# A low-rank update on one core: equal groups of 8 tiles, two spaces for the narrowed copy, and a written order on every engine

## The chip, the cores and the metric

The kernel runs on one core of a Trainium2 chip. A core has TensorE (PE in the profile; PEld is its weight load), VectorE (DVE), ScalarE (ACT), GpSimd (POOL) and SyncE (SP), each with its own instruction queue, 16 DMA engines, and two on-chip memories: SBUF, and PSUM, into which TensorE writes its results. The metric is the device time of one execution in microseconds (us); lower is better.

## The reference

The result is x plus a scaled product of x with two thin matrices (rank 16):

```python
batch, seq, d_model, r = 16, 512, 768, 16
# x: (16, 512, 768) float32, A: (768, 16), B: (16, 768), scale = 0.5
def reference(x, A, B, scale):
    lora = np.matmul(np.matmul(x, A), B)
    return (x + scale * lora).astype(np.float32)
```

There are 8192 rows of 768 numbers. x is 25.17 MB and the output as much, so 50.3 MB cross between the chip's main memory and SBUF.

## The kernel before

**Tiles and parts.** A tile is 128 rows of 768 numbers; there are 64. They come in six parts of 8, 8, 16, 16, 8 and 8 tiles (`PARTS`). A part is loaded into one SBUF space, updated there in place, and stored from there. The spaces are named a, b, c, d; parts 4 and 5 use a and b again (`ROOM`), so they can be loaded only when parts 0 and 1 have been stored. All loads of x and all stores are issued on SP's queue in the order: loads of part 0 (in two halves, `LOADS`), 1, 2 and 3; then stores 0 and 1; then loads 4 and 5, each waiting for the landing of the store that frees its space; then stores 2 to 5. A store waits until every tile of its part is summed.

**The steps of a group.** The work on tiles goes in groups of 4, 12, 16, 16 and 16 (`GROUPS`), and each passes six steps:

1. *narrowed* (L114): four tiles at a time are copied from float32 to float16 into `xh`; ACT and POOL take turns. `xh` is one space of 16 tiles that every group uses again.
2. *turned* (L118): DVE transposes each four tiles of `xh` in place, as 32x32 blocks of 4-byte pairs.
3. *projected* (L129): PE multiplies by A, 24 matmuls per group into one PSUM bank (`ps_yt`); each has 32 columns per tile, so 128, 384 or 512 columns.
4. *spread* (L140): ACT copies the result, scaled, into the diagonal blocks of `y_bd`, four copies per group. There are two `y_bd`, used in turn.
5. *raised* (L150): for two tiles at a time PE multiplies by B, four matmuls into `lora_ps`. A `lora_ps` takes three PSUM banks and there are two of them, so a raise waits for the sum two before it.
6. *added* (L157): DVE adds `lora_ps` to the two tiles of x in place. When a part's last pair is summed, *finished* (L162) issues its store.

Before the first group, A is brought into block form (L97, L102 into `w_bd`) and B is copied four times into `b_mm` (L107), all on DVE.

**What sets the order.** The program is written in an order of its own (the list `order` at L181 mixes turns "t" with sums "a"), and the framework's planner then arranges the instructions of each engine by its own estimates, within what the data allow. In the built program DVE does the four b_mm copies ahead of the transposition of A. For the last two groups it does four sums, two turns, three sums, two turns and the last sum. The projection of the next group follows its last turn.

Of the kernel before, what the change touches and what calls it, by code (L numbers as in the profile page):

```python
# [9 lines left out]
MM_DT = mybir.dt.float16  # L10


PARTS = [8, 8, 16, 16, 8, 8]

ROOM = ["a", "b", "c", "d", "a", "b"]

LOADS = {0: [4, 4]}


GROUPS = [4, 12, 16, 16, 16]  # L20

SUB = 4


@with_exitstack
def kernel(
    ctx: ExitStack,
    tc: tile.TileContext,
    x: bass.AP,
    A: bass.AP,  # L30
    B: bass.AP,
    scale: bass.AP,
    out: bass.AP,
):
    nc = tc.nc
    fp32 = mybir.dt.float32
    P = 128
    Q = 32

    x2 = x.flatten_outer_dims()  # L40
    out2 = out.flatten_outer_dims()
    T, D = x2.shape
    R = A.shape[1]
    NC = D // 64
    GMAX = max(GROUPS)
    assert sum(PARTS) * P == T and sum(GROUPS) == sum(PARTS)
    sc = float(scale)

    const = ctx.enter_context(tc.tile_pool(name="const", bufs=1))
    xpool = ctx.enter_context(tc.tile_pool(name="xp", bufs=1))  # L50
    ypool = ctx.enter_context(tc.tile_pool(name="yp", bufs=1))
    ps_y = ctx.enter_context(tc.tile_pool(name="ps_y", bufs=2, space=bass.MemoryType.PSUM))
    ps_l = ctx.enter_context(tc.tile_pool(name="ps_l", bufs=2, space=bass.MemoryType.PSUM))

    parts = []
    where = []
    tok = 0
    for i, S in enumerate(PARTS):
        parts.append([None, tok, S])
        where += [(i, s) for s in range(S)]  # L60
        tok += S * P

    def rows(t2, i):
        _, tok0, S = parts[i]
        return t2[ds(tok0, S * P), :].rearrange("(p s) d -> p s d", s=S)

    def loaded(i):
        S = parts[i][2]
        t = xpool.tile([P, S, D], fp32, name=f"x_sb{i}", tag=ROOM[i])
        parts[i][0] = t  # L70
        end = 0
        for w in LOADS.get(i, [S]):
            nc.sync.dma_start(out=t[:, ds(end, w), :], in_=rows(x2, i)[:, ds(end, w), :])
            end += w

    a_rows = const.tile([Q, 64 * R], fp32, name="a_rows")
    a_t = const.tile([Q, 2, R, Q], fp32, name="a_t")
    b_f32 = const.tile([R, D], fp32, name="b_f32")  # L80
    w_bd = const.tile([P, NC, 2, P], MM_DT, name="w_bd")
    b_mm = const.tile([P, D], MM_DT, name="b_mm")
    xh = const.tile([P, GMAX, D], MM_DT, name="xh")
    y_bd = [const.tile([P, GMAX, P], MM_DT, name=f"y_bd{i}") for i in range(2)]

    nc.vector.memset(a_rows, 0.0)  # L86
    loaded(0)
    nc.scalar.dma_start(out=b_f32, in_=B)
    nc.scalar.dma_start(out=a_rows[0:NC, :], in_=A.rearrange("(c e) r -> c (e r)", e=64))
    for i in range(1, 4):  # L90
        loaded(i)
    nc.gpsimd.memset(w_bd.rearrange("p c k m -> p (c k m)").bitcast(fp32), 0.0)  # L92
    nc.gpsimd.memset(b_mm.bitcast(fp32), 0.0)  # L93
    for t in y_bd:
        nc.gpsimd.memset(t.rearrange("p s m -> p (s m)").bitcast(fp32), 0.0)  # L95

    nc.vector.transpose(  # L97
        out=a_t.rearrange("i k r c -> i (k r) c"),
        in_=a_rows.rearrange("c (i k r) -> c (k r) i", k=2, r=R),
    )  # L100
    for b in range(P // Q):
        nc.vector.tensor_copy(  # L102
            out=w_bd[ds(b * Q, Q), :, :, ds(b * Q, R)],
            in_=a_t[:, :, :, 0:NC].rearrange("i k r c -> i c k r"),
        )
    for b in range(P // Q):
        nc.vector.tensor_copy(out=b_mm[ds(b * Q, R), :], in_=b_f32)  # L107

    starts = [sum(GROUPS[:g]) for g in range(len(GROUPS))]

    def narrowed(g, q):
        i, s = where[starts[g] + q * SUB]
        engine = nc.gpsimd.tensor_copy if q % 2 else nc.scalar.copy
        engine(out=xh[:, ds(q * SUB, SUB), :], in_=parts[i][0][:, ds(s, SUB), :])  # L114

    def turned(q):
        v = xh[:, ds(q * SUB, SUB), :].bitcast(fp32)
        nc.vector.transpose(out=v, in_=v)  # L118

    state = {}  # L120

    def projected(g, steps):
        n = GROUPS[g]
        if g not in state:
            state[g] = ps_y.tile([P, GMAX * Q], fp32, name="ps_yt")
        xv = xh.rearrange("p s (c j k) -> p s c j k", c=NC, k=2)
        for m in steps:
            c, k = divmod(m, 2)
            nc.tensor.matmul(  # L129
                state[g][:, 0 : n * Q].rearrange("p (s j) -> p s j", j=Q),  # L130
                w_bd[:, c, k, :], xv[:, 0:n, c, :, k],
                start=(m == 0), stop=(m == 2 * NC - 1),
            )

    def spread(g):
        n = GROUPS[g]
        y = state.pop(g).rearrange("p (s j) -> p s j", j=Q)
        for b in range(P // Q):
            q = ds(b * Q, Q)
            nc.scalar.mul(out=y_bd[g % 2][q, 0:n, q], in_=y[q, 0:n, :], mul=sc)  # L140

    lora = {}

    def raised(g, p):
        t = ps_l.tile([P, 2, D], fp32, name="lora_ps")
        lora[g, p] = t
        for h in range(2):
            lhsT = y_bd[g % 2][:, 2 * p + h, :]
            for n0, w in ((0, 512), (512, 256)) if h == 0 else ((0, 256), (256, 512)):
                nc.tensor.matmul(  # L150
                    t[:, h, ds(n0, w)], lhsT, b_mm[:, ds(n0, w)], start=True, stop=True
                )

    def added(g, p):
        i, s = where[starts[g] + 2 * p]
        xs = parts[i][0][:, ds(s, 2), :]
        nc.vector.tensor_tensor(out=xs, in0=xs, in1=lora.pop((g, p)), op=mybir.AluOpType.add)  # L157

    def finished(g, p):
        i, s = where[starts[g] + 2 * p]  # L160
        if s + 2 == PARTS[i]:
            nc.sync.dma_start(out=rows(out2, i), in_=parts[i][0])  # L162
            if i == 1:
                loaded(4)
                loaded(5)

    MMS = 2 * NC
    last = len(GROUPS) - 1
    for q in range(GROUPS[0] // SUB):
        narrowed(0, q)  # L170
        turned(q)
    projected(0, range(MMS))
    spread(0)
    raised(0, 0)
    for g in range(len(GROUPS)):
        pairs = GROUPS[g] // 2
        subs = GROUPS[g + 1] // SUB if g < last else 0
        for q in range(subs):
            narrowed(g + 1, q)

        order = ["a", "a"]  # L181
        p_left, q_left = pairs - 2, subs
        while q_left or p_left:
            if q_left:
                order.append("t")
                q_left -= 1
                if q_left == subs - 1 and q_left and p_left:
                    order.append("t")
                    q_left -= 1
            if p_left:  # L190
                order.append("a")
                p_left -= 1
        p = q = 0
        done = 0
        after = 0
        rest = sum(1 for o in order[max(i for i, o in enumerate(order) if o == "t"):] if o == "a") if subs else 0
        for o in order:
            if o == "t":
                turned(q)
                q += 1  # L200
                continue
            if p + 1 < pairs:
                raised(g, p + 1)
            if q == subs and subs:
                after += 1
                to = min(MMS, -(-MMS * after // max(1, rest - 1)))
                projected(g + 1, range(done, to))
                done = to
            added(g, p)
            finished(g, p)  # L210
            p += 1
        if subs:
            projected(g + 1, range(done, MMS))
            spread(g + 1)
            raised(g + 1, 0)


# [33 lines left out]
```

## Time and profile before

| what | value |
|---|---|
| median of 3 runs | 143.31 us (142.47 to 144.72) |
| the profiled execution | 142.38 us, its span 140.6 us |
| busy: PE, DVE, ACT, POOL | 61.6, 87.5, 35.7, 22.8 us |
| sums (L157) | 32, mean 1.741 us |
| turns (L118) | 16, mean 1.750 us |
| projection matmuls (L129) | 120, 30.4 us in all |
| raising matmuls (L150) | 128, 31.8 us in all |
| narrowing casts on ACT and POOL (L114) | 9 and 7, 2.75 us each |
| first and last store issued | 39.9 and 129.9 us |
| bytes moved by DMA | 50.47 MB, mean 359 GB/s over the span |

The span reaches from the first to the last instruction; the time of an execution is a little longer. The profile's second part cuts the span into 40 slices of 3.5 us: a digit is the busy share of an engine in tenths, and the rows that begin with DMA and GB/s tell how busy the 16 DMA engines were and what they moved. A line of the costliest groups names the source line, the engine, the operation, the tiles and the count; then busy time and mean duration in ns; then how long the engine stood idle just before these instructions and what ended most of that wait. The chain is followed back from the last instruction to whatever released each step. The granted clock is the share of full speed that TensorE was given.

### The profile page before, as it was taken

Reading aid. Unit: us, or ns where it says so; the run is one execution under the profiler, and the core shown is the slowest. Engines: PE = TensorE matmul, PEld = TensorE weight load, DVE = VectorE, ACT = ScalarE, POOL = GpSimd, SP = SyncE. Lnnn points to the kernel's source line nnn. Section 1 sums busy time; section 2 is a strip of 40 time slices with the busy share of each in tenths; the row PEclk is TensorE's granted clock in tenths of the full one; section 3 lists DMA queues with packets and bytes.
Section 4 is the critical chain, followed back from the end, with each engine's and each line's share of the span. In section 5 each row is a group of like instructions: output and inputs, shape, how many; then the busy total and the mean of one; then the engine's idle time right before and its main releaser. Section 6 shows DMA issues by size and latency. Waiting matters only on the chain.

```text
span 140.6 us, 687 instructions
## 1 busy us (share of the span) xinstructions
PE 61.6 (44%) x248; PEld 26.8 (19%) x248; DVE 87.5 (62%) x58; ACT 35.7 (25%) x30; POOL 22.8 (16%) x15
## 2 busy tenths in 40 slices
PE   0000740195553039757049984450709927842000
PEld 0000620042220013223013432220203413320000
DVE  2659059800699991039999771999995008999000
ACT  2070197004960000299000019910000060000000
POOL 8200061004910000292000009400000000000000
PEclk9999999559999856985555799996555895599555
DMA  5999999999999799999998009999005999579992
GB/s 126 382 422 441 447 447 447 447 447 447 447 447 447 336 440 396 413 343 413 447 440 357 0 0 447 447 447 447 0 2 224 433 452 447 238 329 447 447 447 119
DMA packets 1931, 50.47 MB, mean 359 GB/s; under 512 B 236, under 2 KB 236, under 8 KB 264
## 3 DMA queue, kind: packets, MB, share of 16 engines
q1 hardware_dynamic: 1872, 50.33, 84.7%
q10 hardware_dynamic: 56, 0.10, 0.3%
q8 instruction: 2, 0.03, 0.1%
q14 instruction: 1, 0.01, 0.0%
HBM read 25.26 MB, written 25.17 MB: 359 GB/s over the span
## 4 chain that ended last, share of the span: by engine, by line
DVE 51%; PE 25%; ACT 6%; DMA 5%; issue 4%; DVEq 1%; ACTq 0%
DVE x_sb L157 29%; PE ps_yt L129 21%; DVE xh L118 19%; ACT y_bd L140 6%; DMA a_rows<-in_A_dram 5%; PE lora_ps L150 4%; DVE a_t L97 1%; DVE w_bd L102 1%; DVEq L246 1%; DVE a_rows L86 1%; ACTq L246 0%; ACTq L140 0%; DVEq L97 0%; ACTq L114 0%
## 5 line engine op out<-in xcount | busy, mean ns | idle before, releaser
L157 DVE TENSOR_TENSOR x_sb<-x_sb,lora_ps 128x1536 f32<-128x1536 f32 x32 | 54.2, 1741 | 36.8 <-PE lora_ps L150 36.8
L150 PE MATMUL lora_ps<-b_mm,y_bd 128*128 128x512 f16 (+1 forms) x128 | 31.8, 387 | 32.3 <-DVE x_sb L157 21.4
L129 PE MATMUL ps_yt<-xh,w_bd 128*128 128x512 f16 (+2 forms) x120 | 30.4, 424 | 33.5 <-DVE xh L118 33.5
L114 POOL CAST xh<-x_sb 128x3072 f16<-128x3072 f32 x7 | 19.1, 2749 | 66.1 <-PE ps_yt L129 31.8
L140 ACT ACTIVATE y_bd<-ps_yt 32x512 f16<-32x512 f32 (+2 forms) x20 | 10.1, 503 | 73.1 <-PE ps_yt L129 72.9
L118 DVE STREAM_TRANSPOSE xh<-xh 128x1536 f32<-128x1536 f32 x16 | 27.4, 1750 | 0.0
L114 ACT CAST xh<-x_sb 128x3072 f16<-128x3072 f32 x9 | 24.4, 2750 | 4.2 <-DMA x_sb<-in_x_dram 4.1
L150 PEld LDWEIGHTS <-y_bd 128*128 128x128 f16 x128 | 13.6, 110 | 50.4 <-issue 33.9
L129 PEld LDWEIGHTS <-w_bd 128*128 128x128 f16 x120 | 13.2, 119 | 49.8 <-issue 22.7
L107 DVE CAST b_mm<-b_f 16x768 f16<-16x768 f32 x4 | 2.2, 550 | 2.8 <-DMA b_f<-in_B_dram 2.7
L97 DVE STREAM_TRANSPOSE a_t<-a_rows 32x1024 f32<-32x1024 f32 x1 | 1.9, 1932 | 1.6 <-DMA a_rows<-in_A_dram 1.6
L102 DVE CAST w_bd<-a_t 32x384 f16<-32x384 f32 x4 | 1.9, 472 | 0.1
L114 ACT ACT_TABLE_LOAD x1 | 1.3, 1283 | 2.5 <-DVE a_rows L86 2.5
L95 POOL MEMSET y_bd<- 128x1024 f32 x2 | 1.8, 956 | 0.0
L86 DVE MEMSET a_rows<- 32x1024 f32 x1 | 0.9, 912 | 1.0 <-PEq L232 1.0
L92 POOL MEMSET w_bd<- 128x1536 f32 x1 | 1.4, 1378 | 0.3 <-POOLq L232 0.3
L93 POOL MEMSET b_mm<- 128x384 f32 x1 | 0.4, 419 | 0.0
L232 POOL MEMSET const-float32-0.0<- 128x1 f32 x1 | 0.1, 99 | 0.2 <-issue 0.2
L232 POOL MEMSET const-bfloat16-1.0<- 128x1 bf16 x1 | 0.1, 102 | 0.0
L232 POOL MEMSET const-uint8-127<- 128x1 uint8 x1 | 0.1, 102 | 0.0
L232 POOL MEMSET const-float32-1.0<- 128x1 f32 x1 | 0.1, 99 | 0.0
## 6 DMA issues: line engine op xcount, KB each, us to landing
x_sb<-in_x_dram SPq DMA_DIRECT2D x2, 6144.0 KB, 38.1
out_dram<-x_sb SPq DMA_DIRECT2D x4, 3072.0 KB, 10.1
out_dram<-x_sb SPq DMA_DIRECT2D x2, 6144.0 KB, 16.9
x_sb<-in_x_dram SPq DMA_DIRECT2D x3, 3072.0 KB, 16.5
x_sb<-in_x_dram SPq DMA_DIRECT2D x2, 1536.0 KB, 8.7
b_f<-in_B_dram ACTq DMA_DIRECT2D x1, 48.0 KB, 3.8
a_rows<-in_A_dram ACTq DMA_DIRECT2D x1, 48.0 KB
```

The source lines that it names most:

```text
L86: nc.vector.memset(a_rows, 0.0)
L95: nc.gpsimd.memset(t.rearrange("p s m -> p (s m)").bitcast(fp32), 0.0)
L97: nc.vector.transpose(out=a_t.rearrange("i k r c -> i (k r) c"), in_=a_rows.rearrange("c (i k r) -> c (k r) i", k=2, r=R),)
L102: nc.vector.tensor_copy(out=w_bd[ds(b * Q, Q), :, :, ds(b * Q, R)], in_=a_t[:, :, :, 0:NC].rearrange("i k r c -> i c k r"),)
L107: nc.vector.tensor_copy(out=b_mm[ds(b * Q, R), :], in_=b_f32)
L114: engine(out=xh[:, ds(q * SUB, SUB), :], in_=parts[i][0][:, ds(s, SUB), :])
L118: nc.vector.transpose(out=v, in_=v)
L129: nc.tensor.matmul(state[g][:, 0 : n * Q].rearrange("p (s j) -> p s j", j=Q), w_bd[:, c, k, :], xv[:, 0:n, c, :, k], start=(m == 0), stop= ...
L140: nc.scalar.mul(out=y_bd[g % 2][q, 0:n, q], in_=y[q, 0:n, :], mul=sc)
L150: nc.tensor.matmul(t[:, h, ds(n0, w)], lhsT, b_mm[:, ds(n0, w)], start=True, stop=True)
L157: nc.vector.tensor_tensor(out=xs, in0=xs, in1=lora.pop((g, p)), op=mybir.AluOpType.add)
L246: with _tile.TileContext(nc) as tc:
```

## The change

The groups become eight equal ones of 8 tiles. The narrowed copy gets two spaces of 8 tiles, used in turn by even and odd groups, so that it takes as much SBUF as before. Each `y_bd` shrinks to 8 tiles. Part 2 is loaded in two halves of 8 tiles. Above all, from the preparation of A and B onward the planner is switched off (`tc.manual_schedule()`): every engine executes its instructions in the order in which the program writes them. DVE's b_mm copies therefore stand behind those into `w_bd`.

In the written order the casts of a group stand two groups ahead of its sums. DVE does the two turns of group g+1 before the four sums of group g. PE does two raises, then a third of the next group's 24 projection matmuls, a raise, a third, a raise and the last third. The projection matmuls have 256 columns now, and there are 192 in place of 120. The spread of group g+1 follows the sums of group g; on ACT it stands behind the cast of group g+2.

```diff
-LOADS = {0: [4, 4]}
-GROUPS = [4, 12, 16, 16, 16]
+LOADS = {0: [4, 4], 2: [8, 8]}
+GROUP = 8
...
-    xh = const.tile([P, GMAX, D], MM_DT, name="xh")
-    y_bd = [const.tile([P, GMAX, P], MM_DT, name=f"y_bd{i}") for i in range(2)]
+    xh = [const.tile([P, GROUP, D], MM_DT, name=f"xh{i}") for i in range(2)]
+    y_bd = [const.tile([P, GROUP, P], MM_DT, name=f"y_bd{i}") for i in range(2)]
+
+    ctx.enter_context(tc.manual_schedule())
...
+    def narrowed(g):
+        for q in range(GROUP // SUB):
+            i, s = where[g * GROUP + q * SUB]
+            engine = nc.gpsimd.tensor_copy if q % 2 else nc.scalar.copy
+            engine(out=xh[g % 2][:, ds(q * SUB, SUB), :], in_=parts[i][0][:, ds(s, SUB), :])
+
+    def turned(g):
+        for q in range(GROUP // SUB):
+            v = xh[g % 2][:, ds(q * SUB, SUB), :].bitcast(fp32)
+            nc.vector.transpose(out=v, in_=v)
...
+    THIRD = MMS // 3
+    narrowed(0)
+    narrowed(1)
+    turned(0)
     projected(0, range(MMS))
     spread(0)
+    for g in range(NG):
+        more = g + 1 < NG
+        raised(g, 0)
+        raised(g, 1)
+        if g + 2 < NG:
+            narrowed(g + 2)
+        if more:
+            turned(g + 1)
+        added(g, 0)
+        if more:
+            projected(g + 1, range(0, THIRD))
+        raised(g, 2)
+        added(g, 1)
+        if more:
+            projected(g + 1, range(THIRD, 2 * THIRD))
+        raised(g, 3)
+        added(g, 2)
+        if more:
+            projected(g + 1, range(2 * THIRD, MMS))
+        added(g, 3)
+        finished(g)
+        if more:
             spread(g + 1)
```

## The prediction

> **What bounds the kernel now.** I read the page's busy shares, slices and chain first, then the costliest groups, the chain in order of time, and the DMA engines stretch by stretch.
>
> ```profile
> PE 61.6 (44%) x248; PEld 26.8 (19%) x248; DVE 87.5 (62%) x58; ACT 35.7 (25%) x30; POOL 22.8 (16%) x15
> ...
> DVE  2659059800699991039999771999995008999000
> ...
> DMA  5999999999999799999998009999005999579992
> GB/s 126 382 422 441 447 447 447 447 447 447 447 447 447 336 440 396 413 343 413 447 440 357 0 0 447 447 447 447 0 2 224 433 452 447 238 329 447 447 447 119
> ...
> DVE 51%; PE 25%; ACT 6%; DMA 5%; issue 4%; DVEq 1%; ACTq 0%
> DVE x_sb L157 29%; PE ps_yt L129 21%; DVE xh L118 19%; ACT y_bd L140 6%; DMA a_rows<-in_A_dram 5%; PE lora_ps L150 4%; DVE a_t L97 1%; DVE w_bd L102 1%; DVEq L246 1%; DVE a_rows L86 1%; ACTq L246 0%; ACTq L140 0%; DVEq L97 0%; ACTq L114 0%
> ```
>
> No engine is near full: DVE is busiest with 62%. The DMA row is near full up to slice 21 (from 0, 3.5 us each) and then falls to zero twice, in 22 to 23 and 28 to 29; full slices move 447 GB/s. The chain is half DVE (sums L157, turns L118) and a quarter PE, nearly all of it the projection L129.
>
> ```profile
> L157 DVE TENSOR_TENSOR x_sb<-x_sb,lora_ps 128x1536 f32<-128x1536 f32 x32 | 54.2, 1741 | 36.8 <-PE lora_ps L150 36.8
> L150 PE MATMUL lora_ps<-b_mm,y_bd 128*128 128x512 f16 (+1 forms) x128 | 31.8, 387 | 32.3 <-DVE x_sb L157 21.4
> L129 PE MATMUL ps_yt<-xh,w_bd 128*128 128x512 f16 (+2 forms) x120 | 30.4, 424 | 33.5 <-DVE xh L118 33.5
> ...
> L118 DVE STREAM_TRANSPOSE xh<-xh 128x1536 f32<-128x1536 f32 x16 | 27.4, 1750 | 0.0
> L114 ACT CAST xh<-x_sb 128x3072 f16<-128x3072 f32 x9 | 24.4, 2750 | 4.2 <-DMA x_sb<-in_x_dram 4.1
> ```
>
> DVE lost 36.8 us ahead of sums, waiting for the raising matmuls, and PE lost 33.5 us ahead of projections, waiting for DVE's turns. They take turns at waiting. The chain in order of time (start, length, what) shows one such handover whole:
>
> ```profile
> 102.28 3.42 DVE xh L118 x2
> ...
> 105.75 7.36 PE ps_yt L129 x24
> ...
> 113.14 0.59 ACT y_bd L140
> ...
> 115.58 0.84 PE lora_ps L150 x4
> ...
> 116.44 11.74 DVE x_sb L157 x7
> ```
>
> The last turn ends at 105.70, then 24 projection matmuls (7.36 us), the spreading copies (2.4 us) and a raise (0.84 us) pass before DVE adds again at 116.44. DVE had one sum left to fill that time and sat idle for 9.1 us of it. The chain of a group is thus bare once per group. What that costs shows in the DMA queue (busy time by engine, then granted clock, share of the DMA engines, GB/s):
>
> ```profile
> 47.00:76.80 29.80, 16.15 (x51) 6.04 (x52) 20.93 (x13) 7.76 (x6) 5.44 (x2) 0.64 1.00 419
> 76.80:84.90 8.10, 7.15 (x30) 2.98 (x28) 5.50 (x4) 0.91 (x2) 0.89 (x1) 0.86 0.12 49
> 84.90:97.80 12.90, 4.71 (x24) 2.33 (x25) 10.51 (x7) 6.85 (x5) 4.56 (x2) 0.93 1.07 461
> 97.80:108.20 10.40, 5.33 (x14) 1.80 (x14) 9.53 (x6) 0.00 (x0) 0.00 (x0) 0.50 0.00 1
> ...
> 124.00:138.10 14.10, 1.75 (x9) 0.67 (x7) 5.84 (x4) 0.00 (x0) 0.00 (x0) 0.72 1.04 444
> ```
>
> There is no load left to move after 76.8, and a store goes out only when its whole part is summed. A packet is counted where it starts, and one of 48 KB takes 1.76 us at a sixteenth of 447 GB/s (one of 24 KB half of that). So the queue stands still from 77.6 to 84.9, 99.5 to 108.2 and 123.1 to 124.1: 7.3 + 8.7 + 1.0 = 17.0 us. The kernel is bounded by DVE's and PE's alternation from about 77 us on, and by the DMA engines before that.
>
> **The change, part by part.**
>
> *The order on DVE.* Each group of 8 now needs two turns and four sums. Turns that stand behind one another are 1.70 us apart (3.42 for two), sums 1.67 (6.75 for four): 10.1 us a group, as long as nothing is late. Behind the turns of group g+1 stand the four sums of group g, so projection and spreading of g+1 have 6.7 us of sums and then 3.4 us of the turns of g+2 to hide in.
>
> *PE in a group.* Four raises at 0.82 us are 3.3 us. No row has matmuls of 256 columns: 128 columns take 2.72/24 = 0.113 us, and 384 run at 0.164 us apart at full clock, 0.32 at half. So 24 cost between 2.7 and 3.9 us at full clock; I take 3.0, nearer the 128 row since a weight load (0.110 us) lies in each. At half clock, by the 0.427 us spacing of 512 columns at 51.6 us, 24 x 0.427/2 = 5.1 us, and four raises at 1.44 us are 5.8 us. That is 6.3 us a group at full clock, 10.9 at half, against DVE's 10.1. At full clock the last third ends 1.5 us before the last sum does, the spread (four copies between the 268 and 482 ns of the 128 and 384 rows, so 1.1 to 1.9 us, taken 1.5) and a raise end 1.0 us after it, and the turns cover that. In PE's queue the third and fourth raise stand behind projection thirds that wait for the turns; those are done before the first sum starts, so they hold nobody. The shorter groups raise the spreads from 20 copies (10.1 us) to 32 (12.0 us), all on ACT, which is 25% busy.
>
> *Two spaces for the narrowed copy.* POOL waited 31.8 us for projections to leave the single space. Now a cast waits for the projection two groups back, done a group earlier. The cast of g+2 stands ahead of the spread of g+1 on ACT, so a late load also delays that spread. Casts now run beside turns, which no row here shows. Beside sums POOL's casts kept 2.75 us and sums 1.75 us, so I take 0; if the two excluded each other wholly, 2.75 us a group would come on top. It cannot gain: turns alone already take 1.75 us.
>
> *The start.* The planner had put the four b_mm casts (2.24 us) into DVE's wait for A; in written order they stand behind w_bd and end at 14.65 instead of 12.39. The second half of part 0 lands at 11.4 and POOL's cast of it ends at 14.2, so the turns of group 0 run 14.65 to 18.05, its projection to 21. ACT is held by the cast of part 1 (lands 18.8, cast to 21.55), so the spread ends at 23.1. DVE turns group 1 from 21.6 to 25.0 and adds until 31.7. The first store, issued at 39.9 before, goes out at about 32.
>
> *Part 2 in two loads.* One more issue on SP (0.42 us), and the first half lands at about (18.8 + 33.9)/2 = 26.4, midway between part 1 and the whole of part 2; cast by 29.2, needed at 31.7. Without it group 2 would wait 5 us.
>
> *From there.* DVE ends groups 1 to 4 at 41.8, 51.9, 62.0 and 72.1. Group 4 needs part 3, which lands at 48.1, cast 50.9, needed 51.9: no wait. Loads 4 and 5 wait on SP for the landings of stores 0 and 1. The DMA queue serves in order (store 0, issued at 39.93, moved only when the loads were through at 47, and landed at 55.0), so an earlier issue does not bring load 4 in before the 71.1 of now. Its cast ends at 73.85, DVE waits 1.8 us; groups 5, 6, 7 end at 84, 94 and 102.
>
> *The transfers, which set the end.* Stores go out at 32, 42, 64 (behind load 5's issue on SP), 84, 94 and 102. Until 76.8 the queue carries what it carries now, without a hole. Then 18.87 MB of stores remain, and the queue gets to them at 77, 91, 105 and 112: each is issued 7 to 13 us before its turn. So the three gaps go and nothing is late next but the queue itself. Sum by gaps: 140.6 - 17.0 = 123.6. Sum by pace: 18.87 MB at 447 GB/s (slices of full stores) is 42.2 us, from 77.6 to 119.8, and 1.6 us from last byte to the end of the span as now: 121.4. I take the middle, 122.5. The profiled execution of before took 142.38, 1.78 over its span, so **124.3 us**. It was 0.9 under the median of 143.31; the forecast lies 13% under either, and 2% is about what a measurement here tells from no change. At the 418 GB/s of the stretch that mixes loads and stores, 18.87 MB take 45.1 us and the time is 126.1; at the 461 of 84.9 to 97.8 it is 122.
>
> **Rivals.**
>
> *The clock stays half and PE sets the pace.* Granted clock in two stretches:
>
> ```profile
> 62.00:79.00 17.00, 10.46 (x30) 3.69 (x28) 16.71 (x10) 4.59 (x2) 2.25 (x1) 0.50 0.87 372
> 79.00:96.10 17.10, 9.66 (x49) 4.53 (x48) 12.32 (x8) 7.76 (x6) 5.44 (x2) 1.00 0.75 322
> ```
>
> The clock was half for 17 us while PE was busy 62% of them, and full in the next 17 us with 56%: it depends on how idle time is placed. It fell at 62.0 after 2.5 us of idleness. The new order has 62% at full clock, with holes of 1.5 to 1.7 us. If it falls, a group takes 10.9 us of PE plus the bare spread of 1.6: 12.5. If all groups do so, DVE ends at 21.6 + 8 x 12.5 = 121.6, and 10.7 us from the last store's issue to the end as now (140.6 - 129.9): 132.3, **134 us**. Against it: at half clock PE would be busy 87% of the time, and such a stretch (120 to 123.4) was followed by full clock. Up to 1.2 us more a group is covered by the 7 us ahead of store 3. A full exclusion of casts and turns comes to the same place: 21.6 + 8 x 12.9 + 10.7 + 1.8 = 137.
>
> *The transfers keep a mean of 359 GB/s.* That is the page's mean over the span; if it were a ceiling of the memory, 50.47 MB would take 140.6 us and nothing would change: **142 us**. The Trainium skill, in "DMA: Bandwidth & Descriptors", section "Where 436 GB/s comes from", says just this, that between HBM and SBUF the memory side binds, at about 358 GB/s a core; by that the change gains nothing. The trace disagrees: 419 GB/s over the 29.8 us from 47.0, 461 in 84.9 to 97.8, 444 in 124.0 to 138.1.
>
> *Slower: the group's steps stay bare in written order.* PE's queue holds the raises behind thirds that wait for turns, and ACT's holds the spread behind a cast that may wait for a load. If turns, projection at half clock, spread, raise and the first two sums followed each other, a group would take 3.4 + 5.1 + 1.5 + 1.4 + 3.3 = 14.7 us; from 87.3 to 116.4 before took 29.1 us for 16 tiles, 14.6 for 8. Then 21.6 + 8 x 14.6 + 10.7 + 1.8 = **151 us**. It decides from 13.5 us a group on: 21.6 + 8 x 13.5 = 129.6 is when DVE ends now. For it: 51 of the first 130 us ran at half clock. Against it: casts are due a whole group early but for load 4, and the turns no longer wait for sums.
>
> That the change does not do what it says is excluded on DVE: in the built program two turns stand ahead of each four sums.
>
> **How the numbers follow.** Full DMA queue, 122 to 127: 0.74. Half clock or blocked casts, in part or all along, 127 to 137: 0.17. The 359 GB/s ceiling: 0.04. Bare steps, slower: 0.03. The rest, 0.02, is faster than 122. The range of 121.5 to 131 takes in the first case and the nearer half of the second. Faster by over 2%: 0.93; within: 0.04; slower: 0.03.
>
> **What would show it.** The DMA row at nines from slice 1 to the last but one, with no gap over 1 us; the first store issued near 32 and the last near 102; DVE's idle time before sums down from 36.8 to under 8 us; a period of about 10.1 us between groups; load 4 landing near 71 with a short wait of DVE behind it; turns still at 1.75 us beside casts. Wrong would be a period over 11.3 us (store 3 late for the queue), transfers under 418 GB/s once stores follow each other, or the clock at half for most of the span.

## The result

The changed kernel takes 125.28 us (median of 4 runs, 124.99 to 125.44) against 143.16 us before: 0.876 of the time, 95% interval 0.872 to 0.880. The forecast was 124.3, and the time lies inside its range. The profiled execution took 125.14 us, its span 123.3.

The page of the changed kernel, with the rows that answer to those shown of before:

```profile
PE 51.8 (42%) x320; PEld 32.3 (26%) x320; DVE 89.8 (73%) x58; ACT 35.3 (29%) x41; POOL 25.1 (20%) x16
...
DVE  2019997826999999999989999999998499000000
...
DMA  4999999999998897999999999989989989999980
GB/s 73 398 371 466 406 454 414 454 430 391 510 510 383 383 499 335 430 414 454 414 446 422 422 454 507 407 383 494 449 351 478 478 351 446 391 438 438 414 375 32
...
DVE 57%; PE 12%; issue 6%; DMA 5%; ACT 2%; DVEq 1%; ACTq 0%
```

The DMA row has no zero left before its last slice: it is at nine, or close to it, from slice 1 to slice 38. DVE is busy 73% of the span in place of 62%, and from slice 11 to slice 30 it hardly stops. PE's busy time fell by 9.8 us although it does the same multiplications. The chain now ends with DVE's last sum and 57% of it is DVE, but that is not what binds: the last store was issued at 105.15 and landed 17.4 us later, because the queue had other stores to move first.

The costliest groups of the changed kernel:

```profile
L155 DVE TENSOR_TENSOR x_sb<-x_sb,lora_ps 128x1536 f32<-128x1536 f32 x32 | 54.0, 1741 | 6.2 <-PE lora_ps L148 6.2
L129 PE MATMUL ps_yt<-xh,w_bd 128*128 128x256 f16 x192 | 28.8, 299 | 31.1 <-DVE xh L119 31.1
L148 PE MATMUL lora_ps<-b_mm,y_bd 128*128 128x512 f16 (+1 forms) x128 | 26.1, 338 | 19.7 <-ACT y_bd L138 13.8
...
L119 DVE STREAM_TRANSPOSE xh<-xh 128x1536 f32<-128x1536 f32 x16 | 27.4, 1754 | 1.0 <-ACT xh L114 1.0
```

The wait that bound the kernel, DVE ahead of its sums, fell from 36.8 to 6.2 us. PE still waits 31.1 us for turns, of which 21.1 us is the start; the rest comes in pieces of up to 1.8 us while DVE does the turns.

DVE in the changed kernel, in order of time (start, length, what, count):

```profile
35.46 3.43 DVE L119 STREAM_TRANSPOSE xh<-xh 128x1536 f32<-128x1536 f32 x2
38.82 6.71 DVE L155 TENSOR_TENSOR x_sb<-x_sb,lora_ps 128x1536 f32<-128x1536 f32 x4
45.45 3.42 DVE L119 STREAM_TRANSPOSE xh<-xh 128x1536 f32<-128x1536 f32 x2
48.79 6.71 DVE L155 TENSOR_TENSOR x_sb<-x_sb,lora_ps 128x1536 f32<-128x1536 f32 x4
55.42 3.42 DVE L119 STREAM_TRANSPOSE xh<-xh 128x1536 f32<-128x1536 f32 x2
58.77 5.05 DVE L155 TENSOR_TENSOR x_sb<-x_sb,lora_ps 128x1536 f32<-128x1536 f32 x3
```

Sums start at 38.82, 48.79 and 58.77: a group takes 9.97 us, with no idle time shown between its pieces.

The DMA engines of the changed kernel, stretch by stretch (busy time by engine, granted clock, DMA share, GB/s):

```profile
4.00:46.00 42.00, 17.04 (x106) 11.05 (x107) 32.56 (x24) 15.51 (x16) 11.25 (x4) 1.00 1.03 438
...
48.00:76.00 28.00, 17.43 (x112) 11.05 (x111) 27.50 (x18) 12.62 (x15) 8.25 (x3) 0.94 1.01 433
76.00:104.00 28.00, 16.22 (x96) 9.60 (x96) 25.72 (x17) 5.89 (x10) 2.75 (x1) 0.94 1.03 443
```

In three long stretches the queue moved 433 to 443 GB/s, whether loads, loads mixed with stores, or stores alone.

### The profile page after: what moved, and what is told of

Read it like the earlier page. It is cut to its first block, busy times and chain, and to the rows that moved or that the text cites. A ratio compares the mean times of both kernels' runs of the same rounds, so it can differ in the third digit from the quotient of the medians.

```text
span 123.3 us, 854 instructions
## 1 busy us (share of the span) xinstructions
PE 51.8 (42%) x320; PEld 32.3 (26%) x320; DVE 89.8 (73%) x58; ACT 35.3 (29%) x41; POOL 25.1 (20%) x16
## 4 chain that ended last, share of the span: by engine, by line
DVE 57%; PE 12%; issue 6%; DMA 5%; ACT 2%; DVEq 1%; ACTq 0%
DVE x_sb L155 31%; DVE xh L119 19%; PE ps_yt L129 8%; DMA a_rows<-in_A_dram 5%; PE lora_ps L148 5%; DVE w_bd L103 3%; ACT y_bd L138 2%; DVE b_mm L108 2%; DVE a_t L98 2%; DVEq L225 1%; DVE a_rows L87 1%; ACTq L225 0%; ACTq L138 0%; DVEq L103 0%; DVEq L98 0%
## 5 line engine op out<-in xcount | busy, mean ns | idle before, releaser
L129 PE MATMUL ps_yt<-xh,w_bd 128*128 128x256 f16 x192 | 28.8, 299 | 31.1 <-DVE xh L119 31.1
L148 PE MATMUL lora_ps<-b_mm,y_bd 128*128 128x512 f16 (+1 forms) x128 | 26.1, 338 | 19.7 <-ACT y_bd L138 13.8
L114 POOL CAST xh<-x_sb 128x3072 f16<-128x3072 f32 x8 | 22.2, 2781 | 56.2 <-DMA x_sb<-in_x_dram 49.7
L129 PEld LDWEIGHTS <-w_bd 128*128 128x128 f16 x192 | 20.2, 105 | 39.4 <-issue 33.3
L114 ACT CAST xh<-x_sb 128x3072 f16<-128x3072 f32 x8 | 22.0, 2752 | 23.8 <-DMA x_sb<-in_x_dram 23.7
L138 ACT ACTIVATE y_bd<-ps_yt 32x256 f16<-32x256 f32 x32 | 12.0, 375 | 35.9 <-PE ps_yt L129 35.3
L148 PEld LDWEIGHTS <-y_bd 128*128 128x128 f16 x128 | 12.1, 100 | 30.6 <-ACT y_bd L138 16.1
L103 DVE CAST w_bd<-a_t 32x384 f16<-32x384 f32 x4 | 4.3, 1087 | 0.1
L96 POOL MEMSET y_bd<- 128x512 f32 x2 | 1.0, 528 | 0.0
## 6 DMA issues: line engine op xcount, KB each, us to landing
x_sb<-in_x_dram SPq DMA_DIRECT2D x1, 6144.0 KB, 45.6
```

The source lines that it names most:

```text
L103: nc.vector.tensor_copy(out=w_bd[ds(b * Q, Q), :, :, ds(b * Q, R)], in_=a_t[:, :, :, 0:NC].rearrange("i k r c -> i c k r"),)
L114: engine(out=xh[g % 2][:, ds(q * SUB, SUB), :], in_=parts[i][0][:, ds(s, SUB), :])
L129: nc.tensor.matmul(y_ps[g], w_bd[:, c, k, :], xv[:, :, c, :, k], start=(m == 0), stop=(m == 2 * NC - 1),)
L138: nc.scalar.mul(out=y_bd[g % 2][q, :, q], in_=y[q, :, :], mul=sc)
L148: nc.tensor.matmul(t[:, h, ds(n0, w)], lhsT, b_mm[:, ds(n0, w)], start=True, stop=True)
```

## The experiments

The kernel before was run beside each set; its medians there were 144.0 (the first four runs), 143.3 (the next four) and 143.3 us (the last four). Ratios are to those.

### Is the queue now the only bound?

The first run keeps the loads of x and the stores in SP's order and leaves out everything else, the small loads of A and B too, so its output is x itself:

```diff
     for i in range(1, 4):
         loaded(i)
... (removed: preparation, casts, turns, matmuls, spreads and sums of all groups)
+    for i in range(len(PARTS)):
+        nc.sync.dma_start(out=rows(out2, i), in_=parts[i][0])
+        if i == 1:
+            loaded(4)
+            loaded(5)
```

> The changed kernel's loads and stores in its order on SP's queue, and nothing else: no cast, turn, matmul or sum, so the output is x itself. Theory (from the first load on the DMA queue alone sets the time of the changed kernel): 123 to 126 us, within 2% of its 125.3. Rival (DVE's chain of groups still sets part of it): under 120 us, since no store waits for a sum here.

Measured: 123.01 us (122.94 to 123.06). All the computing of the changed kernel thus adds 2.3 us to its bare transfers; before it added about 20. The theory holds.

The second run issues the stores on ACT's queue:

```diff
-        nc.sync.dma_start(out=rows(out2, i), in_=parts[i][0])
+        nc.scalar.dma_start(out=rows(out2, i), in_=parts[i][0])
```

> As the run with the transfers alone, but the stores are issued on ACT's queue, so that loads and stores no longer stand in one line; the output is x itself. Theory (the 16 DMA engines' pace binds, at about 438 GB/s): the same within 1%, 123 to 126 us. Rival (one queue leaves holes where one transfer follows another): 2 to 5% quicker, 117 to 122 us.

Measured: 123.20 us (123.06 to 123.31). A second queue closes no holes, so the bound is not that loads and stores stand in one line. What is left is the pace at which the 16 engines move the data; whether the engines or the memory behind them set that pace was not tried.

### How much delay of DVE does the queue cover?

An unused tile is turned once more behind each group's two turns, once 512 numbers wide, once 1536:

```diff
+    pad = const.tile([P, 512], fp32, name="pad")    # 1536 in the second run
...
             nc.vector.transpose(out=v, in_=v)
+        nc.vector.transpose(out=pad, in_=pad)
```

> The changed kernel with one more turn of an unused tile of 512 numbers behind each group's two turns, about 0.6 us of DVE time, 4.8 us in all. Theory (the DMA queue sets the end and store 3 is issued 5.4 us before its turn): it is late by 0.6 x 7 = 4.2 us, still covered, 125 to 126 us. Rival (DVE sets the end): 130 us.

> The same with one full turn (1536 numbers) more in each group, 1.7 us, 13.4 us in all, a period of 11.7 us. Theory (queue, 5.4 us of cover at store 3): store 3 is 11.9 us late, a hole of 6.5 us, and all later stores stay covered: 131 to 133 us. Rival (DVE sets the end): 138 to 139 us. Rival (DVE is far from mattering): 125 to 126 us.

Measured: 125.19 us (124.96 to 125.60) and 128.93 us (128.22 to 130.40). The small delay costs nothing. The large one costs about 3.5 us of the 13.4 that DVE was given; the expected 131 to 133 was too high. DVE and the queue in that run, from two views, show why:

```profile
27.51 6.75 DVE L159 TENSOR_TENSOR x_sb<-x_sb,lora_ps 128x1536 f32<-128x1536 f32 x4 [0.67 <-PE lora_ps L152]
...
87.72 5.04 DVE L159 TENSOR_TENSOR x_sb<-x_sb,lora_ps 128x1536 f32<-128x1536 f32 x3
93.22 1.75 DVE L159 TENSOR_TENSOR x_sb<-x_sb,lora_ps 128x1536 f32<-128x1536 f32 x1 [0.46 <-PE lora_ps L152]
```

```profile
91.50:95.00 3.50, 2.57 (x18) 1.66 (x16) 3.04 (x3) 0.78 (x3) 0.00 (x0) 0.88 0.03 14
95.00:125.00 30.00, 11.00 (x56) 6.10 (x56) 18.46 (x11) 2.22 (x6) 0.00 (x0) 0.74 0.98 419
```

The hole is there, but it is 3.5 us long and not 6.5. Store 3 was issued at 95.01 and not at 97.9. Of the seven added turns ahead of it the first two fell into waits that DVE has at the start of the changed kernel anyway (0.98 us ahead of its second pair of turns, 3.42 us ahead of its first sums), and the first sums started at 27.51 here, before the 28.80 there. From then on five added turns cost 10.2 us, a little more than their 8.5. The cover at store 3 was sized rightly; the delay was not.

### What closed the gaps: order, spaces or group size?

Three parts of the change were undone one at a time, the place of the turns in two ways. In the kernel before, groups of 8 were made alone, and then together with a second space.

The planner left on:

```diff
-    ctx.enter_context(tc.manual_schedule())
```

> The changed program with the planner left on, so that groups of 8, two spaces and the written program stay and only the order on the engines is the planner's: it does the b_mm copies first and does the turns of two groups in a row ahead of eight sums. Theory (turns ahead of the neighbour's sums keep the queue fed, whoever orders them): 125 to 129 us. Rival (the gain comes from the hand-written order on each engine): 135 us or more.

Measured: 125.45 us (124.97 to 126.58), ratio 0.875 [0.867, 0.883]. Switching the planner off is worth nothing that can be measured: given this program it also sets turns ahead of sums.

The turns of the next group behind the four sums:

```diff
-        if more:
-            turned(g + 1)
         added(g, 0)
...
         added(g, 3)
         finished(g)
         if more:
+            turned(g + 1)
+            projected(g + 1, range(MMS))
             spread(g + 1)
```

> The changed kernel with the two turns, the whole projection of the next group and its spread moved behind the four sums. Theory (the gain comes from hiding projection, spread and raise behind sums): a group takes 6.7 + 3.4 + 2.7 to 5.1 + 1.6 + 0.8 to 1.4 = 15.2 to 18.2 us, DVE ends at 28 + 7 x that + 6.7, and 12.5 us come behind it: 154 to 175 us, slower than the kernel before. Rival (small groups, two spaces and the split load bring the gain): under 135 us.

Measured: 164.27 to 168.11 us in four runs, ratio 1.144 [1.131, 1.157]. DVE waits 7.1 to 7.4 us for a raise in each group of the middle of this run. With the whole chain bare once in every 8 tiles the small groups are a loss.

The turns between the second and the third sum:

```diff
+        added(g, 0)
+        raised(g, 2)
+        added(g, 1)
+        raised(g, 3)
         if more:
             turned(g + 1)
-        added(g, 0)
... (removed: the sums, raises and thirds that followed here)
+            projected(g + 1, range(MMS))
         added(g, 2)
...
         added(g, 3)
```

> The changed kernel, two spaces and written order, with the turns of the next group between the second and the third sum and the whole projection behind them, as the program of the kernel before has them. Theory (with two spaces the place of the turns decides): only two sums, 3.4 us, lie over projection, spread and raise (5.1 us at full clock, 8.1 at half), so a group takes 12 to 15 us; DVE ends near 119 to 139, 131 to 151 us. Rival (two spaces are enough wherever the turns stand): within 2% of 125.3.

Measured: 142.08 us, ratio 0.992 [0.988, 0.996]. Two sums don't cover the chain. From DVE's order of time in this run, where the bracket gives its idle time and what ended it:

```profile
69.16 3.42 DVE L155 TENSOR_TENSOR x_sb<-x_sb,lora_ps 128x1536 f32<-128x1536 f32 x2 [3.62 <-PE lora_ps L148]
72.49 3.43 DVE L119 STREAM_TRANSPOSE xh<-xh 128x1536 f32<-128x1536 f32 x2
75.84 3.38 DVE L155 TENSOR_TENSOR x_sb<-x_sb,lora_ps 128x1536 f32<-128x1536 f32 x2
82.83 3.42 DVE L155 TENSOR_TENSOR x_sb<-x_sb,lora_ps 128x1536 f32<-128x1536 f32 x2 [3.60 <-PE lora_ps L148]
```

DVE waits 3.6 us for a raise once a group, and a group takes 13.67 us.

One space for the narrowed copy, with the turns left ahead. The casts of a group must then follow the projection of the one before it:

```diff
-    xh = [const.tile([P, GROUP, D], MM_DT, name=f"xh{i}") for i in range(2)]
+    xh = [const.tile([P, GROUP, D], MM_DT, name=f"xh{i}") for i in range(1)]
...
-        if g + 2 < NG:
-            narrowed(g + 2)
...
             spread(g + 1)
+            if g + 2 < NG:
+                narrowed(g + 2)
```

> The changed kernel with one space of 8 tiles for the narrowed copy: the casts of the next group follow the projection of the one before it, and on ACT they follow its spread. Theory (the two spaces take the casts off the chain): turns wait for a cast that ends 2.9 us after the last sum, 13 us a group, sums of group 0 from about 34: DVE ends near 127, 137 to 141 us. Rival (the order of turns and sums alone brings the gain): within 2% of 125.3.

Measured: 143.36 us, ratio 0.998 [0.992, 1.003]: the whole gain is gone, a little more than expected. DVE in order of time in this run:

```profile
71.15 3.44 DVE L119 STREAM_TRANSPOSE xh<-xh 128x1536 f32<-128x1536 f32 x2 [3.48 <-ACT xh L114]
74.51 6.85 DVE L155 TENSOR_TENSOR x_sb<-x_sb,lora_ps 128x1536 f32<-128x1536 f32 x4
84.85 3.44 DVE L119 STREAM_TRANSPOSE xh<-xh 128x1536 f32<-128x1536 f32 x2 [3.48 <-ACT xh L114]
```

Now the turns of each group wait 3.48 us for ACT's cast, and a group takes 13.7 us again. Not all of that wait comes from the space, as ACT shows ahead of the turn at 71.15:

```profile
66.81 1.54 ACT L138 ACTIVATE y_bd<-ps_yt 32x256 f16<-32x256 f32 x4 [9.42 <-PE ps_yt L129]
...
68.37 2.75 ACT L114 CAST xh<-x_sb 128x3072 f16<-128x3072 f32 x1
```

The projection is done by 66.8, and the cast then stands 1.54 us behind the spread on ACT. About 1.9 us of the wait is what the one space costs by itself; the other 1.5 us is this order on ACT. With the cast first the turns could start some 1.5 us earlier in each group, roughly 10 us over seven groups. That is an estimate from these rows; the run was not made, so 143.36 us is the time of one space in this order and not the best that one space can give.

The kernel before with groups of 8, and then with two spaces as well:

```diff
-GROUPS = [4, 12, 16, 16, 16]
+GROUPS = [8] * 8
```

> The kernel before with groups of 8 and nothing else changed: one space, its own order, the planner. Theory (small groups alone bring little, since a cast must wait for the one space and the turns stand between two and two sums): 12.6 to 15.6 us a group, 134 to 145 us. Rival (small equal groups alone bring the gain, because stores go out in smaller steps): 130 us or less.

```diff
-    xh = const.tile([P, GMAX, D], MM_DT, name="xh")
+    xhs = [const.tile([P, GMAX, D], MM_DT, name=f"xh{i}") for i in range(2)]
...
-        engine(out=xh[:, ds(q * SUB, SUB), :], in_=parts[i][0][:, ds(s, SUB), :])
+        engine(out=xhs[g % 2][:, ds(q * SUB, SUB), :], in_=parts[i][0][:, ds(s, SUB), :])
... (turns and projection use xhs[g % 2] too)
```

> The kernel before with groups of 8 and two spaces for the narrowed copy, its own program and the planner. In the built order the planner now sets most turns ahead of all the sums of the group to the left. Theory (a second space lets turns go ahead, and whoever orders them feeds the queue): 125 to 130 us. Rival (the order written by hand is needed): 135 to 145 us.

Measured: 142.85 us, ratio 0.987 [0.977, 0.997], and 131.00 us, ratio 0.913 [0.908, 0.918]. Group size alone brings about 1% at most, which is not clear of the noise here. With the second space the old program gains two thirds of what the change gains. The 131.0 lies just outside the 125 to 130 expected. In its built order some turns still stand between two sums of the same group, which is the likely rest; that was read from the order and not tried by itself.

Put together, with groups of 8 throughout:

| | turns ahead of the sums | turns between the sums |
|---|---|---|
| two spaces | 125.3 (125.5 with the planner) | 142.1 |
| one space | 143.4 | 142.9 (old program, planner) |

The 131.0 us has no place in the table, since there the planner moved most turns but not all. In these runs either half alone gains 1% at most, and both together gain 12%. With one missing, DVE waits about 3.5 us once per group, for a cast or for a raise; the two waits are of nearly the same size, so taking away one leaves the other. That they come out so nearly equal is in part the order on ACT with one space, as said above: turns ahead of the sums may be worth something with one space too.

### The start, and the load in halves

Both casts of group 0 on ACT, and the b_mm copies ahead of the transposition of A:

```diff
+    for b in range(P // Q):
+        nc.vector.tensor_copy(out=b_mm[ds(b * Q, R), :], in_=b_f32)
     nc.vector.transpose(
         out=a_t.rearrange("i k r c -> i (k r) c"),
...
-    for b in range(P // Q):
-        nc.vector.tensor_copy(out=b_mm[ds(b * Q, R), :], in_=b_f32)
...
-            engine = nc.gpsimd.tensor_copy if q % 2 else nc.scalar.copy
+            engine = nc.gpsimd.tensor_copy if q % 2 and g else nc.scalar.copy
```

> The changed kernel with the four b_mm copies ahead of the transposition of A again and both casts of group 0 on ACT, so that no POOL cast runs beside DVE's copies into w_bd. Theory (the start is late because a POOL cast and a DVE copy out of SBUF shut each other out, and because of the order of the b_mm copies; all of it is covered by the queue): the four copies into w_bd take 1.9 us in all as in the kernel before, the first sum starts near 25.4 instead of 28.8, the time stays within 1% of 125.3. Rival (what delays those copies is not POOL): they take 4.3 us again.

Measured: 125.41 us (125.33 to 125.45). The changed kernel's start on DVE and POOL:

```profile
10.83 4.39 DVE L103 CAST w_bd<-a_t 32x384 f16<-32x384 f32 x4
15.25 2.24 DVE L108 CAST b_mm<-b_f 16x768 f16<-16x768 f32 x4
...
28.80 6.75 DVE L155 TENSOR_TENSOR x_sb<-x_sb,lora_ps 128x1536 f32<-128x1536 f32 x4 [3.42 <-PE lora_ps L148]
```

```profile
11.88 3.00 POOL L114 CAST xh<-x_sb 128x3072 f16<-128x3072 f32 x1 [8.48 <-DMA x_sb<-in_x_dram]
19.18 2.75 POOL L114 CAST xh<-x_sb 128x3072 f16<-128x3072 f32 x1 [4.30 <-DMA x_sb<-in_x_dram]
```

From the chain in order of time, the last two copies into w_bd, the second of which met POOL's cast, and a projection at the start and late in the run:

```profile
11.80 0.47 DVE w_bd L103
12.28 2.93 DVE w_bd L103
...
21.11 5.12 PE ps_yt L129 x24
...
94.89 0.91 PE ps_yt L129 x8
```

And DVE's start in the experiment:

```profile
10.69 1.94 DVE L105 CAST w_bd<-a_t 32x384 f16<-32x384 f32 x4
12.66 3.65 DVE L119 STREAM_TRANSPOSE xh<-xh 128x1536 f32<-128x1536 f32 x2
...
25.21 6.71 DVE L155 TENSOR_TENSOR x_sb<-x_sb,lora_ps 128x1536 f32<-128x1536 f32 x4
```

Without a POOL cast beside them the copies into w_bd take 1.94 us in place of 4.39. This run also moved the b_mm copies, but their place is not the cause: in the kernel before with groups of 8, where they stand first and POOL casts beside the copies into w_bd, these took 4.39 us again. And in the run with the large delay POOL's first cast met the b_mm copies instead: they took 4.68 us in place of 2.24, and the copies into w_bd 1.95. The first sum starts at 25.21 instead of 28.80, and the time does not move: 3.6 us at the start are covered.

Part 2 loaded whole:

```diff
-LOADS = {0: [4, 4], 2: [8, 8]}
+LOADS = {0: [4, 4]}
```

> The changed kernel with part 2 loaded whole. Theory (stores are issued well ahead of their turn): group 2's casts end near 36.7 instead of 30.7, its turns wait about 1.2 us, the time stays within 1% of 125.3. Rival (the split is needed): 128 us or more.

Measured: 125.48 us (125.19 to 125.63). The turns of group 2 waited 0.59 us for their cast, where the prediction had 5 us, mostly because DVE came to them late. The split is not needed.

## Why the prediction was right

**The bound and the end.** The forecast rested on one statement: the three holes in the DMA queue close and nothing but the queue is late next. The page shows the holes gone, the transfers alone take 123.0 us, and 0.6 us of delay per group costs nothing. The sum was 1.0 us short. Its two ways gave 123.6 and 121.4 for the span, the middle was taken, and 123.3 came out. The term that was too small is in the sum by pace: it moved the stores from 77 us on at 447 GB/s, and from 76.8 to 121.5 the queue moved 411. The sum by gaps came within 0.3 us, but partly by luck: it took the first 77 us as unchanged and the rest at the old pace, while by 76.8 us 32.1 MB had been moved in place of 31.5, and the rest went slower.

**The period.** 10.1 us was forecast, 9.97 measured. Spreads were taken at 1.5 us for four and took 1.57 (375 ns each). Full-clock projections were taken at 3.0 us for 24; eight took 0.91 us late in the run, so 2.7. That no row had matmuls of 256 columns was misread: half of the raising matmuls are of that width (64 in the kernel before, mean 319 ns over both clocks).

**Two spaces.** The cost of casts beside turns was bounded by 0 and 2.75 us and taken as 0. Turns averaged 1.754 us against 1.750 before, so 0 was right. The prediction gave the second space a short paragraph and the order on DVE the long one; in the runs made neither was worth more than 1% without the other.

**The start, the step that was wrong.** The first sum was forecast at 25.0 and came at 28.80, the first store at 32 and came at 35.57. Two terms were too small. The copies into w_bd took 4.39 us instead of 1.93, since POOL now casts beside them; the prediction had asked whether casts and turns exclude each other, but not casts and copies. And the first projection took 5.1 us instead of 2.9: the row of 128 columns, 0.113 us a matmul, was read as full clock, and it is the pace of half clock. Its weight loads took 144 ns (median), as in the changed kernel's first projection, against 95 ns late in the run. The prediction's own price for half clock, 5.1 us, was right. Neither reached the end, as the run with the quicker start shows.

**Stores and load 4.** Stores were issued at 35.6, 45.6, 66.1, 86.1, 96.7 and 105.2 instead of 32, 42, 64, 84, 94 and 102, all ahead of their turn. Load 4 let ACT cast at 71.29, as forecast; DVE did not wait the 1.8 us for it, because it was later itself.

**The rivals.** After the first projection and up to PE's last matmul the clock stayed full but for two stretches of 3.4 us, and the sums that waited for a raise there lost 0.5 and 0.6 us. A ceiling of 359 GB/s was not there: the mean over the span is 409 and the long stretches run at 433 to 443, so the 358 GB/s of the Trainium skill's "DMA: Bandwidth & Descriptors", "Where 436 GB/s comes from", does not bind on this core in these runs. The rival on the slow side named 13.5 us a group as the point from which the time is that of before; the runs with one space and with turns between the sums had 13.7 us and came out at 143.4 and 142.1. Its price was right, its condition did not arise.

## What to carry to other kernels

When two engines wait for each other once per group, look for every wait that closes the loop: here the buffer and the order each held about 3.5 us, and removing one alone showed 1% at most. Then ask what the transfers alone would take, and run just that: it tells how much is left, and when to stop. Delay that falls ahead of a full queue is free as long as the next store still comes before its turn, so an early step may be misjudged by several microseconds without moving the time.

## What the runs showed of the hardware

- A POOL cast and a DVE copy from SBUF to SBUF shut each other out: the copy into w_bd that met POOL's cast took 2.93 us instead of 0.47, and that cast 3.00 us instead of 2.75 (12.28 to 15.21 for the copy, 11.88 to 14.88 for the cast). DVE's turns and sums beside POOL casts kept their times. The Trainium skill, "SBUF — State Buffer", section "Who interferes with whom", says so of copies and casts on DVE in a mode that uses two ports, while an instruction with one SBUF input outside those modes is free of it; the trace agrees with both in the times, though the mode of an instruction doesn't show in it.
- The granted clock reads full up to the first change that the profile records (to full, at 25.9 us), but the first projection ran at half up to there: 24 matmuls of 256 columns took 5.1 us, 0.21 us each, while eight took 0.91 us late in the run, 0.11 each (both lines are shown with the experiment on the start). In the kernel before the first recorded change, also to full, is at 17.6 us, behind its first projection. The Trainium skill, "TensorE: Matmul & The Clock Gate", Part 1, says that the throttled state is the default and activity releases it, which fits. The mean clock of a profile's page is too high by this.
- The changed kernel's last packets start one or two at a time between 119.5 and 121.5, while with the transfers alone nearly all have started by 119.0. By 104 us the changed kernel had moved only about 0.15 MB less than that run, some 0.35 us of the queue's time, so most of the remaining 2.3 us lies in this tail; why the engines end unevenly was not tried.
